# Hybrid RWKV-7 / GLA layer: the inverse of the 32x32 diagonal blocks moved from VectorE to GpSimd, with one packed transpose, and lower right-hand sides carried through a matmul by an identity

## Chip, cores and metric

One core of one Trainium2 chip. The metric is the device time of one execution of the whole program in microseconds, the median over several runs. What a run leaves beside the time is a profile of one execution.

## The reference

One decoder layer on 2048 tokens of width 1024: an RMS norm, one input projection of 3248 columns, two mixers side by side on its columns (RWKV-7 with 8 heads of 64, and gated linear attention with 4 heads), an output projection with residual, a second norm, a SwiGLU feed-forward network of width 2816 with residual, and a last norm. The change touches the RWKV-7 mixer, whose recurrence over the tokens is, for each head,

```python
def step(S, inp):
    r_t, w_t, k_t, v_t, a_t, b_t = inp
    sa = jnp.einsum('bhvk,bhk->bhv', S, a_t)
    S = (S * w_t[:, :, None, :] + sa[..., None] * b_t[:, :, None, :]
         + v_t[..., None] * k_t[:, :, None, :])
    y = jnp.einsum('bhvk,bhk->bhv', S, r_t)
    return S, y
```

with a decay `w`, `a = -kk` (the normed key) and `b = kk * iclr`. All of it is in fp32.

## The kernel before, in words

**Two phases.** Phase A (0 to about 1340 us) is the input projection and both mixers, in four blocks of 512 tokens. Phase B (`phase_b`) is the output projection and the feed-forward network; the change doesn't touch it.

**Phase A.** A block has 8 chunks of 64 tokens, and its 8 RWKV heads go in 4 head pairs, 128 channels to a pair: 16 pairs in the four blocks. Five streams of work exist: `z` (the projection: `weights` loads a 128-column tile of the weight and splits it, ScalarE writes the high part `w_hi` on L371 and GpSimd the low part `w_lo` on L372; `zmm` runs 24 matmuls into the PSUM tile `zd`, of which there are two; `shift` and `shifted` mix in the token before, with two small GpSimd copies on L390 and L393), `a` (`stage_a`: from r, k and v of a pair to the scores `e` and `ra`), `a2` (`stage_a2`, below), `b` (`stage_b`: the chain over a pair's 8 chunks, whose steps on VectorE are `uv` on L695 and two updates of the state `S` on L703) and `g` (the gated attention, `gmix`, with a copy of its state to `gss` on GpSimd, L822). Each stream is a generator that yields an estimated time after each piece of work; `run` merges the five by these times, and the framework's scheduler then settles the order of the instructions on each engine from the merged program. Within an engine the order is fixed when the program is built: an instruction that waits holds up all that stand behind it on that engine.

**Chunked form.** Within a chunk the recurrence is a triangular system: `I - E` with the 64x64 strictly triangular `E` of the scores has to be inverted and applied to the right-hand sides `R` (two halves: the scaled `a` and a product with `v`). For a pair there are 16 such matrices (8 chunks, 2 heads), in `e`. `stage_a2` treats each as 2x2 blocks of 32: it inverts the two diagonal blocks, and does a block substitution with matmuls.

**The inverse of the diagonal blocks (L597 to L626).** Four transposes on VectorE of 32x32 squares (L597, one for each group of 32 partitions) write `ln`; each reads the elements repeated four times, so that a lane has 1024 elements. Then `lm` is set to an identity by a GpSimd copy (L601), and 31 substitution steps follow, j from 31 down to 1. Each is two instructions on VectorE, `lt = lm[j] * ln` (L606) and `lm = lm + lt` (L608), on 128 lanes with j x (8 - j // 4) elements each; each needs the result of the one before it:

```python
for j in range(31, 0, -1):
    i0 = j // 4
    n = 8 - i0
```

After the step j = 8 the matmuls for the right-hand sides are issued (`atp`, L615, and `upp`, L622, whose results ScalarE copies into `R`). A VectorE transpose of `lm` then gives the inverses `ui` (L626).

**The block substitution.** X and R are the same tile. For the upper 32 rows of a chunk X = T R (matmuls `xu` on L640, ScalarE copies on L644). The upper rows, times the lower left block of `e` (matmuls `xy` on L648, contraction over 32 rows), are added to the lower rows of R by VectorE (L653). The lower rows are then multiplied by their own inverse (`xl` on L657, ScalarE copies on L661). At the end the part of X for `a` is transposed back (`wtp`) for `stage_b`.

Of the kernel before, what the change touches and what calls it, by code (L numbers as in the profile page):

```python
# [11 lines left out]
F32 = mybir.dt.float32  # L12
# [4 lines left out]
ALU = mybir.AluOpType  # L17
PSUM = bass.MemoryType.PSUM
DRAM = bass.MemoryType.DRAM

D = 1024
# [13 lines left out]
# column tiles of the input projection  # L35
ZR, ZK, ZV, ZL, ZG, ZQ, ZKG, ZVG, ZOG = 0, 4, 8, 12, 13, 14, 16, 18, 22

# columns of the per-channel vectors
# [3 lines left out]
# columns of the constant block  # L42
# [23 lines left out]
class K:  # L66
# [16 lines left out]
    def rsqrt(self, x, n, name):  # L83
        """1/sqrt(x) for a small [128, n] tile: integer first guess, three Newton steps."""
        nc = self.nc
        y = self.small.tile([128, n], F32, name=name + "_y")
        t = self.small.tile([128, n], F32, name=name + "_t")
        nc.vector.tensor_scalar(out=y.bitcast(I32), in0=x.bitcast(I32), scalar1=-0.5, scalar2=float(0x5F3759DF),
                                op0=ALU.mult, op1=ALU.add)
        for _ in range(3):  # L90
            nc.vector.tensor_tensor(out=t, in0=y, in1=y, op=ALU.mult)
            nc.vector.scalar_tensor_tensor(out=t, in0=t, scalar=-0.5, in1=x, op0=ALU.mult, op1=ALU.mult)
            nc.vector.scalar_tensor_tensor(out=y, in0=t, scalar=1.5, in1=y, op0=ALU.add, op1=ALU.mult)
        return y

    # A step y -> (x y y - 3 s s) y takes s / sqrt(x) to -2 s^3 / sqrt(x): the scales that end in 1.
# [4 lines left out]
    def row_rs(self, ss, keep=None):  # L101
        """1/rms of 128 rows from two partial sums of squares."""
        nc = self.nc
        x = self.small.tile([128, 1], F32, name="rn_x")
        nc.vector.tensor_tensor(out=x, in0=ss[:, 0:1], in1=ss[:, 1:2], op=ALU.add)
        nc.vector.tensor_scalar(out=x, in0=x, scalar1=1.0 / D, scalar2=RMS_EPS, op0=ALU.mult, op1=ALU.add)
        y = (keep or self.small).tile([128, 1], F32, name="rn_y", bufs=16 if keep else 2)
        t = self.small.tile([128, 1], F32, name="rn_t")
        nc.vector.tensor_scalar(out=y.bitcast(I32), in0=x.bitcast(I32), scalar1=-0.5, scalar2=-554047172.0,
                                op0=ALU.mult, op1=ALU.add)  # L110
        for sc in (self.S0, self.S1, self.S2):
            nc.vector.scalar_tensor_tensor(out=t, in0=x, scalar=y, in1=y, op0=ALU.mult, op1=ALU.mult)
            nc.vector.scalar_tensor_tensor(out=y, in0=t, scalar=-3.0 * sc * sc, in1=y, op0=ALU.add, op1=ALU.mult)
        return y

    def row_scale(self, x, junk, keep=None):
        """1/rms of the rows of a [128, D] tile."""
        nc = self.nc
        ss = self.small.tile([128, 2], F32, name="rn_ss")
        for i in range(2):  # L120
            nc.scalar.activation(out=junk, in_=x[:, i * 512:i * 512 + 512], func=AF.Square, accum_out=ss[:, i:i + 1])
        return self.row_rs(ss, keep)

# [1 line left out]
    def phase_a(self, ctx):  # L125
# [34 lines left out]
        # persistent state  # L160
# [21 lines left out]
    def stacks(self):  # L182
        nc = self.nc
        # up-projections: rows [hi; lo; hi] against data [hi; hi; lo] (and the like)
# [15 lines left out]
    def run(self):  # L200
        """Emits the blocks' work as streams that are merged by estimated time."""
# [27 lines left out]
    @staticmethod  # L229
    def some(gen, n):  # L230
        """The next n timed steps of a stream."""
        for r in gen:
            yield r
            n -= isinstance(r, float)
            if not n:
                return
# [37 lines left out]
    def xcols(self, b, kp):  # L274
        """256 columns of a block's rows."""
# [3 lines left out]
    def nstat0(self):  # L279
        """1/rms of the first block's rows, from the tiles that nprep goes on with."""  # L280
# [16 lines left out]
    def nstat(self, b):  # L297
        """1/rms of the block's rows."""
# [10 lines left out]
    def nprep(self, b):  # L309
        """the block's normed rows, channel-major, in hi and lo parts, 256 channels a tile."""  # L310
# [50 lines left out]
    def weights(self, ct):  # L361
        """128 columns of the input projection, in hi and lo parts."""
# [12 lines left out]
    def zmm(self, ct):  # L375
        """z^T of one 128-column tile of the input projection, [128, BLK] in PSUM."""
# [9 lines left out]
    def shift(self, ps, i, rows=128):  # L386
        """mu-weighted copy of z, one token late; the last column is kept for the next block."""
# [66 lines left out]
    def stage_a(self, b, hp):  # L454
        """From r, k, v of one head pair to everything that the chain over its chunks needs."""
# [12 lines left out]
        # decay  # L468
# [45 lines left out]
        # [b|k] (even chunk) and [k|b] (odd chunk), divided by the running decay  # L514
# [3 lines left out]
        # r and a of the two chunks, times the running decay; T a comes to the places before and after r  # L518
# [6 lines left out]
        # scores  # L525
# [18 lines left out]
        # token-major [b;k]  # L544
# [9 lines left out]
        # token-major centred v (chunks of a pair swapped)  # L554
# [13 lines left out]
        # bonus * v  # L568
# [17 lines left out]
    def stage_a2(self, b, hp):  # L586
        """Applies the inverse of I - E to the right-hand sides [a | A_ak v]."""
# [4 lines left out]
        # inverses of the 32x32 diagonal blocks of I - E, one per lane and four rows  # L592
        ln = s.tile([128, 32, 32], F32, name="ln", bufs=1)
        for q in range(4):
            par, t0 = q // 2, 32 * (q % 2)
            ev = e.rearrange("p h a x t -> p (h a) x t")[32 * q:32 * q + 32, :, par, t0:t0 + 32]
            nc.vector.transpose(out=ln[32 * q:32 * q + 32],  # L597
                                in_=ev.rearrange("p a t -> p t a").unsqueeze(2).to_broadcast([32, 32, 4, 8]))
# [4 lines left out]
        for j in range(31, 0, -1):  # L603
            i0 = j // 4
            n = 8 - i0
            nc.vector.tensor_tensor(out=lt[:, 0:j, i0:], in0=lm[:, j:j + 1, i0:].to_broadcast([128, j, n]),  # L606
                                    in1=ln[:, j, 0:j].unsqueeze(2).to_broadcast([128, j, n]), op=ALU.mult)
            nc.vector.tensor_tensor(out=lm[:, 0:j, i0:], in0=lm[:, 0:j, i0:], in1=lt[:, 0:j, i0:], op=ALU.add)  # L608
            yield 0.6
            if j == 8:  # L610
                # right-hand sides, token-major, pairs of chunks on the partitions
# [16 lines left out]
        # X = T R by blocks of 32  # L628
# [17 lines left out]
        for g in G2:  # L646
            ps = self.mb("xy", [128, 2, 2, 2, 64])
            each(ps, g, lambda ps, i, j, h, par: nc.tensor.matmul(  # L648
                out=ps[lw(par), i, :, h, :], lhsT=e[up(par), h, j, par, 32:64], rhs=X[up(par), j, :, h, :],
                start=True, stop=True))  # L650
            for par in range(2):
                Rg = R[lw(par), 2 * g:2 * g + 2]
                nc.vector.tensor_tensor(out=Rg, in0=ps[lw(par)], in1=Rg, op=ALU.add)  # L653
# [18 lines left out]
    def stage_b(self, b, hp):  # L672
        """The chain over the chunks of one head pair, group norm, bonus and gate."""
# [7 lines left out]
        for c in range(NCH):  # L681
# [10 lines left out]
            # T a S in the chunk's own rows, r S in the other rows  # L692
# [22 lines left out]
        # group norm (y is centred), gain, bonus, gate  # L715
# [84 lines left out]
    def gmix(self, b, jj):  # L800
# [4 lines left out]
        # token-major k  # L805
# [6 lines left out]
        # chunk states  # L812
# [18 lines left out]
        for h in range(2):  # L831
            hq = slice(64 * h, 64 * h + 64)
            # scores
# [41 lines left out]
    # tiles of phase B take the slots that phase A's tags leave  # L875
# [29 lines left out]
    def phase_b(self):  # L905
# [10 lines left out]
        def prep(half, nb, kps=range(KT // 2)):  # L916
            """normed rows of 512 tokens, channel-major, in hi and lo parts."""
# [25 lines left out]
        # output projection and residual  # L943
# [118 lines left out]
def layout(inp):  # L1062
    """Lays the inputs out for the kernel: tiles, padding and per-channel columns."""
# [60 lines left out]
```

## Time and profile before

| quantity | value |
|---|---|
| median of 3 runs | 3018.58 us (3017.28 to 3021.06) |
| span of the profiled execution | 3011.3 us |
| TensorE busy (matmuls) | 2871.0 us (95% of the span) |
| VectorE busy | 1732.7 us (58%) |
| ScalarE busy | 953.1 us (32%) |
| GpSimd busy | 344.2 us (11%) |
| DMA | 206.08 MB, 68 GB/s over the span |

The span is the time between the first and the last instruction in the profile of one execution; the times of the runs hold what lies around it as well. A share is an average over two phases that differ: of 40 slices of the span, the first 17 or 18 are phase A, with VectorE at six to eight tenths, and the rest phase B, with VectorE at three to five tenths and TensorE at nine or more. So a stage is to be read in its own stretch. PE is TensorE (PEld its loading of weights), DVE is VectorE, ACT ScalarE, POOL GpSimd, SP the engine that issues the DMAs. The clock is the granted share of TensorE's full clock.

### The profile page before, as it was taken

What the parts mean: (1) busy time and instruction counts of PE and PEld (TensorE: products, weight loads), DVE (VectorE), ACT (ScalarE), POOL (GpSimd) and SP (SyncE); (2) the same over time, 40 slices, a digit from 0 to 9 for tenths busy, and PEclk for the clock granted to TensorE, in tenths of its full rate; (3) what the DMA queues carried; (4) which work ended last, traced back from release to release, by engine and by line L of the source; (5) the groups of instructions that cost most, each with busy time, mean ns of one, the idle gap of its engine ahead of it and who ended that gap; (6) DMA issues with size and microseconds to landing.
All of it is one profiled execution on the core that took longest, in us unless ns stands there. A gap on an engine that the chain in (4) does not pass through costs nothing.

```text
span 3011.3 us, 38996 instructions
## 1 busy us (share of the span) xinstructions
PE 2871.0 (95%) x15112; PEld 2247.0 (75%) x15112; DVE 1732.7 (58%) x3990; ACT 953.1 (32%) x1718; POOL 344.2 (11%) x451
## 2 busy tenths in 40 slices
PE   7898999899898989899999999999999999999998
PEld 5676677666666767668878888888888888888886
DVE  6868797888888897874433333333355333333334
ACT  5444445444445445332321111111132111111112
POOL 4222232213322222200000000000000000000000
PEclk9999989989999999989999999999999999999999
DMA  3122111221122111135531111111134111111111
GB/s 108 48 71 78 50 53 47 78 67 56 53 67 81 53 53 50 57 114 175 180 119 45 54 42 42 50 55 50 42 126 138 52 42 42 51 54 50 42 42 57
DMA packets 99033, 206.08 MB, mean 68 GB/s; under 512 B 8608, under 2 KB 41600, under 8 KB 98848
## 3 DMA queue, kind: packets, MB, share of 16 engines
q1 hardware_dynamic: 98848, 203.59, 21.7%
q8 instruction: 119, 1.95, 0.3%
q14 instruction: 66, 0.54, 0.1%
HBM read 178.39 MB, written 25.17 MB: 68 GB/s over the span
## 4 chain that ended last, share of the span: by engine, by line
PE 76%; DVE 20%; issue 2%; ACT 1%; DMA 1%; POOL 0%; SPq 0%; DVEq 0%; ACTq 0%; POOLq 0%
PE ups L995 5%; PE ups L996 5%; PE gps L996 5%; PE gps L997 5%; PE gps L995 5%; PE ups L997 5%; PE dn L1018 5%; PE dn L1019 5%; PE dn L1017 5%; DVE ln L597 3%; PE zd L383 3%; DVE lm L608 3%; PE zd L381 3%; PE zd L382 3%; DVE lt L606 3%
## 5 line engine op out<-in xcount | busy, mean ns | idle before, releaser
L381 PE MATMUL zd<-nh,w_hi 128*128 128x512 f32 x832 | 353.9, 426 | 0.8 <-DVE gkk L777 0.6
L383 PE MATMUL zd<-nh,w_lo 128*128 128x512 f32 x832 | 349.2, 420 | 0.0
L1020 DVE TENSOR_TENSOR h<-dn,h 128x512 f32<-128x512 f32 x352 | 242.7, 690 | 180.6 <-PE dn L1019 180.5
L382 PE MATMUL zd<-nl,w_hi 128*128 128x512 f32 x832 | 345.6, 415 | 0.0
L372 POOL TENSOR_TENSOR w_lo<-w_raw,w_hi 128x512 fp32r<-128x512 f32 x208 | 273.8, 1322 | 614.5 <-ACT w_hi L371 571.8
L1000 DVE TENSOR_TENSOR sgu<-sgu,ups 128x512 f32<-128x512 f32 x88 | 60.2, 684 | 392.6 <-PE ups L997 390.4
L1018 PE MATMUL dn<-wdl,hh 128*128 128x512 f32 x704 | 278.4, 395 | 0.0
L996 PE MATMUL gps<-n2l,wgh 128*128 128x512 f32 x704 | 278.2, 395 | 0.0
L995 PE MATMUL gps<-n2h,wgh 128*128 128x512 f32 x704 | 277.6, 394 | 0.4 <-ACT wgh L901 0.4
L996 PE MATMUL ups<-n2l,wuh 128*128 128x512 f32 x704 | 278.0, 395 | 0.0
L995 PE MATMUL ups<-n2h,wuh 128*128 128x512 f32 x704 | 277.7, 394 | 0.2 <-ACT wuh L901 0.2
L1019 PE MATMUL dn<-wdh,hl 128*128 128x512 f32 x704 | 277.7, 395 | 0.0
L997 PE MATMUL gps<-n2h,wgl 128*128 128x512 f32 x704 | 277.4, 394 | 0.0
L997 PE MATMUL ups<-n2h,wul 128*128 128x512 f32 x704 | 277.4, 394 | 0.0
L1017 PE MATMUL dn<-wdh,hh 128*128 128x512 f32 x704 | 277.4, 394 | 0.0
L901 ACT CAST wdh<-raw 128x1024 fp32r<-128x1024 f32 x44 | 46.4, 1053 | 462.5 <-PE dn L1019 250.5
L383 PEld LDWEIGHTS zd<-nh,w_lo 128*128 128x128 f32 x832 | 161.6, 194 | 35.7 <-issue 7.5
L381 PEld LDWEIGHTS zd<-nh,w_hi 128*128 128x128 f32 x832 | 162.5, 195 | 33.2 <-issue 5.2
L382 PEld LDWEIGHTS zd<-nl,w_hi 128*128 128x128 f32 x832 | 161.9, 195 | 33.3 <-issue 7.9
L371 ACT CAST w_hi<-w_raw 128x512 fp32r<-128x512 f32 x208 | 126.3, 614 | 130.9 <-PE zd L382 83.7
L999 ACT ACTIVATE sgu<-gps 128x512 f32<-128x512 f32 x88 | 52.7, 599 | 339.4 <-PE gps L997 339.4
L995 PEld LDWEIGHTS gps<-n2h,wgh 128*128 128x128 f32 x704 | 132.1, 188 | 33.0 <-ACT wgh L901 0.9
(244 smaller groups left out, 5111.9 us busy)
## 6 DMA issues: line engine op xcount, KB each, us to landing
w_raw<-in_win SPq DMA_DIRECT2D x208, 256.0 KB, 2.7
raw<-in_wg SPq DMA_DIRECT2D x44, 512.0 KB, 4.2
raw<-in_wu SPq DMA_DIRECT2D x44, 512.0 KB, 3.6
raw<-in_wd SPq DMA_DIRECT2D x44, 512.0 KB, 3.6
xk<-in_x SPq DMA_DIRECT2D x16, 512.0 KB, 4.6
raw<-mix SPq DMA_DIRECT2D x16, 512.0 KB, 3.6
hx<-in_x SPq DMA_DIRECT2D x16, 512.0 KB, 3.6
hs<-hx SPq DMA_DIRECT2D x16, 512.0 KB, 2.9
```

What stands on the lines that cost most here:

```text
L371: nc.scalar.copy(out=whi[:, ks, :], in_=raw)
L372: nc.gpsimd.tensor_tensor(out=wlo[:, ks, :], in0=raw, in1=whi[:, ks, :].bitcast(F32), op=ALU.subtract)
L381: nc.tensor.matmul(out=ps, lhsT=whi[:, k, :], rhs=self.nh[k], start=(k == 0), stop=False)
L382: nc.tensor.matmul(out=ps, lhsT=whi[:, k, :], rhs=self.nl[k], start=False, stop=False)
L383: nc.tensor.matmul(out=ps, lhsT=wlo[:, k, :], rhs=self.nh[k], start=False, stop=(k == KT - 1))
L995: nc.tensor.matmul(out=ps, lhsT=w[0][:, ks], rhs=h, start=(k == 0), stop=False)
L996: nc.tensor.matmul(out=ps, lhsT=w[0][:, ks], rhs=l, start=False, stop=False)
L997: nc.tensor.matmul(out=ps, lhsT=w[1][:, ks], rhs=h, start=False, stop=(k == KT - 1))
L1017: nc.tensor.matmul(out=ps, lhsT=hh[:, ts], rhs=wd[f][0][:, ds], start=(f == 0), stop=False)
L1018: nc.tensor.matmul(out=ps, lhsT=hh[:, ts], rhs=wd[f][1][:, ds], start=False, stop=False)
L1019: nc.tensor.matmul(out=ps, lhsT=hl[:, ts], rhs=wd[f][0][:, ds], start=False, stop=(f == 1))
L1020: nc.vector.tensor_tensor(out=H[t][:, ds], in0=ps, in1=H[t][:, ds], op=ALU.add)
```

## The change

- The four transposes of a pair become one. ScalarE first copies the four diagonal squares into a packed tile `ed` (four copies of 32 partitions x 256 elements; `ed` takes the slot of `lt`), and one VectorE transpose on 128 lanes, which reads `ed` with the same fourfold repetition, writes `ln`.
- All 62 substitution instructions of a pair are issued on GpSimd; the operations, their operands and their order are the same.
- Two GpSimd copies for each pair write a 32x32 identity over the lower diagonal squares of `e`, once the squares are in `ed`. The matmul `xy` then contracts over all 64 rows of a chunk, the upper rows of X through the lower left block and the lower rows of R through the identity, so that its result is already the sum. ScalarE copies it into R, in place of VectorE's addition.

```diff
@@ -584,18 +584,24 @@
         yield (f"a1{b}.{hp}",)
     def stage_a2(self, b, hp):
         nc, s = self.nc, self.s
         yield f"a1{b}.{hp}"
         Pm, art, e, ra, bkt, uv, bv = self.ab.pop((b, hp))
         ars = art[:, 1:].rearrange("p (a x) t -> p a x t", x=4)
-        ln = s.tile([128, 32, 32], F32, name="ln", bufs=1)
+        ed = s.tile([128, 32, 8], F32, name="ed", tag="lt", bufs=1)
         for q in range(4):
             par, t0 = q // 2, 32 * (q % 2)
             ev = e.rearrange("p h a x t -> p (h a) x t")[32 * q:32 * q + 32, :, par, t0:t0 + 32]
-            nc.vector.transpose(out=ln[32 * q:32 * q + 32],
-                                in_=ev.rearrange("p a t -> p t a").unsqueeze(2).to_broadcast([32, 32, 4, 8]))
+            nc.scalar.copy(out=ed[32 * q:32 * q + 32], in_=ev.rearrange("p a t -> p t a"))
+        ln = s.tile([128, 32, 32], F32, name="ln", bufs=1)
+        nc.vector.transpose(out=ln, in_=ed.unsqueeze(2).to_broadcast([128, 32, 4, 8]))
+        for par in range(2):
+            q = slice(64 * par + 32, 64 * par + 64)
+            nc.gpsimd.tensor_copy(out=e.rearrange("p h a x t -> p (h a) x t")[q, :, par, 32:64],
+                                  in_=self.ident[q, q].unsqueeze(1).to_broadcast([32, 8, 32]))
         yield 4.0
         lm = s.tile([128, 32, 8], F32, name="lm", bufs=1)
         nc.gpsimd.tensor_copy(out=lm, in_=self.dlt.rearrange("p (k i) -> p k i", i=8))
@@ -603,12 +609,12 @@
         for j in range(31, 0, -1):
             i0 = j // 4
             n = 8 - i0
-            nc.vector.tensor_tensor(out=lt[:, 0:j, i0:], in0=lm[:, j:j + 1, i0:].to_broadcast([128, j, n]),
+            nc.gpsimd.tensor_tensor(out=lt[:, 0:j, i0:], in0=lm[:, j:j + 1, i0:].to_broadcast([128, j, n]),
                                     in1=ln[:, j, 0:j].unsqueeze(2).to_broadcast([128, j, n]), op=ALU.mult)
-            nc.vector.tensor_tensor(out=lm[:, 0:j, i0:], in0=lm[:, 0:j, i0:], in1=lt[:, 0:j, i0:], op=ALU.add)
+            nc.gpsimd.tensor_tensor(out=lm[:, 0:j, i0:], in0=lm[:, 0:j, i0:], in1=lt[:, 0:j, i0:], op=ALU.add)
             yield 0.6
             if j == 8:
                 R = s.tile([128, NPR, 2, 2, 64], F32, name="R", bufs=2)
                 atp = self.mb("atp", [128, NPR, 128])
                 for i in range(NPR):
@@ -625,7 +631,7 @@
         ui = s.tile([128, 8, 32], F32, name="ui", bufs=1)
         nc.vector.transpose(out=ui.rearrange("p a (i x) -> p i x a", x=4), in_=lm.rearrange("p k i -> p i k"))
         yield 0.5
         X = R
         up = lambda par: slice(64 * par, 64 * par + 32)
         lw = lambda par: slice(64 * par + 32, 64 * par + 64)
@@ -646,11 +652,10 @@
         for g in G2:
             ps = self.mb("xy", [128, 2, 2, 2, 64])
             each(ps, g, lambda ps, i, j, h, par: nc.tensor.matmul(
-                out=ps[lw(par), i, :, h, :], lhsT=e[up(par), h, j, par, 32:64], rhs=X[up(par), j, :, h, :],
-                start=True, stop=True))
+                out=ps[lw(par), i, :, h, :], lhsT=e[64 * par:64 * par + 64, h, j, par, 32:64],
+                rhs=X[64 * par:64 * par + 64, j, :, h, :], start=True, stop=True))
             for par in range(2):
-                Rg = R[lw(par), 2 * g:2 * g + 2]
-                nc.vector.tensor_tensor(out=Rg, in0=ps[lw(par)], in1=Rg, op=ALU.add)
+                nc.scalar.copy(out=R[lw(par), 2 * g:2 * g + 2], in_=ps[lw(par)])
             yield 1.5
         for g in G2:
             ps = self.mb("xl", [128, 2, 2, 2, 64])
```

Lines of the changed program have numbers that are 2 to 6 higher from `stage_a2` on (it also leaves out the comments): L599 is the packed transpose, L603 the identity copies, L612 and L614 the substitution, L632 the transpose to `ui`, L658 the copy that replaces the addition, L700 and L708 `stage_b`'s `uv` and `S`, L827 the copy of `gss`.

**How the order moves.** The first place is VectorE in the second block of tokens, second pair: behind the last score eviction of `stage_a` (`e`, `ra`). Before, this stretch has the end of the first pair's substitution with its `ui`, the four transposes of the second pair, and the beginning of the second pair's substitution:

```order
L606 TENSOR_TENSOR lt<-lm,ln 128x8
L608 TENSOR_TENSOR lm<-lm,lt 128x8
L597 STREAM_TRANSPOSE ln<-e 32x1024
L626 STREAM_TRANSPOSE ui<-lm 128x32x8
L597 STREAM_TRANSPOSE ln<-e 32x1024 x3
L606 TENSOR_TENSOR lt<-lm,ln 128x31
L608 TENSOR_TENSOR lm<-lm,lt 128x31
L653 TENSOR_TENSOR R<-xy,R 32x512 x4
L606 TENSOR_TENSOR lt<-lm,ln 128x30
L608 TENSOR_TENSOR lm<-lm,lt 128x30
L606 TENSOR_TENSOR lt<-lm,ln 128x29
```

In the changed program, from that eviction on, with the second pair's own `ui`:

```order
L539 TENSOR_TENSOR e<-scp,cst 128x4x64
L541 TENSOR_TENSOR ra<-scp,cst 128x256
L599 STREAM_TRANSPOSE ln<-ed 128x1024
L632 STREAM_TRANSPOSE ui<-lm 128x32x8
L700 TENSOR_TENSOR uv<-yp,R 64x128
L708 SCALAR_TENSOR_TENSOR S_1_101<-ch,Pm_120,st 64x64 x2
L700 TENSOR_TENSOR uv<-yp,R 64x128
L708 SCALAR_TENSOR_TENSOR S_0_100<-ch,Pm_120,st 64x64 x2
```

The packed transpose and the one of `ui` now stand directly behind one another, and the steps of `stage_b` (`uv`, `S`) come behind `ui`.

The second place is VectorE in the first pair of the same block, behind the score evictions. Before:

```order
L597 STREAM_TRANSPOSE ln<-e 32x1024 x2
L606 TENSOR_TENSOR lt<-lm,ln 128x31
L608 TENSOR_TENSOR lm<-lm,lt 128x31
L606 TENSOR_TENSOR lt<-lm,ln 128x30
L608 TENSOR_TENSOR lm<-lm,lt 128x30
L606 TENSOR_TENSOR lt<-lm,ln 128x29
L398 SCALAR_TENSOR_TENSOR r<-zd,om,sh 128x512
L580 TENSOR_TENSOR bv<-bp,v 128x4x64 x2
L695 TENSOR_TENSOR uv<-yp,R 64x128
L608 TENSOR_TENSOR lm<-lm,lt 128x29
L606 TENSOR_TENSOR lt<-lm,ln 128x28
L608 TENSOR_TENSOR lm<-lm,lt 128x28
```

In the changed program:

```order
L599 STREAM_TRANSPOSE ln<-ed 128x1024
L708 SCALAR_TENSOR_TENSOR S_1_113<-ch,Pm_122,st 64x64 x2
L398 SCALAR_TENSOR_TENSOR r<-zd,om,sh 128x512
L580 TENSOR_TENSOR bv<-bp,v 128x4x64 x2
L700 TENSOR_TENSOR uv<-yp,R 64x128
L708 SCALAR_TENSOR_TENSOR S_0_112<-ch,Pm_122,st 64x64 x2
L718 TENSOR_TENSOR y<-yp,y 64x256 x2
L724 TENSOR_REDUCE va<-ysq 128x8
L726 TENSOR_SCALAR va<-va 128x8
L88 TENSOR_SCALAR gn_y<-va 128x8
L632 STREAM_TRANSPOSE ui<-lm 128x32x8
L91 TENSOR_TENSOR gn_t<-gn_y 128x8
```

Here work of the projection (`r`), of `stage_a` (`bv`) and of `stage_b` stands between the packed transpose and `ui`.

The third place is GpSimd in the third pair of the same block. Before (memsets for `uv`, the low parts of weights, the state copy of the gated attention, and the carry of the token shift):

```order
L563 MEMSET uv 64x2x128
L372 TENSOR_TENSOR w_lo<-w_raw,w_hi 128x512
L822 COPY gss<-SG_118 128x128
L372 TENSOR_TENSOR w_lo<-w_raw,w_hi 128x512
L393 COPY cr<-sh 128x1
L372 TENSOR_TENSOR w_lo<-w_raw,w_hi 128x512
```

In the changed program:

```order
L603 COPY e<-ident 32x8x32
L562 MEMSET uv 64x2x128
L563 MEMSET uv 64x2x128
L372 TENSOR_TENSOR w_lo<-w_raw,w_hi 128x512
L603 COPY e<-ident 32x8x32
L827 COPY gss<-SG_118 128x128
L612 TENSOR_TENSOR lt<-lm,ln 128x31
L614 TENSOR_TENSOR lm<-lm,lt 128x31
L612 TENSOR_TENSOR lt<-lm,ln 128x30
L614 TENSOR_TENSOR lm<-lm,lt 128x30
```

The copy of `gss` stands ahead of the substitution, and weights' low parts stand around it.

## Rows read from the trace of the kernel before

**Rows 1.** The page, its first line
```profile
span 3011.3 us, 38996 instructions
```

**Rows 2.** Stretches: length, busy us (count) of PE, PEld, DVE, ACT, POOL, clock, DMA
```profile
60.00:1260.00 1200.00, 1097.76 (x7232) 823.12 (x7231) 983.82 (x2605) 552.43 (x1059) 318.55 (x397) 0.95 0.20 61
1260.00:1340.00 80.00, 71.61 (x465) 52.38 (x464) 60.79 (x184) 31.70 (x60) 0.61 (x2) 0.85 0.30 94
```

**Rows 3.** Busy time by stretches of 10 us, same columns
```profile
60.00:70.00 10.00, 8.23 (x59) 6.29 (x58) 9.96 (x17) 3.52 (x6) 5.41 (x5) 1.00 0.28 80
430.00:440.00 10.00, 6.14 (x40) 4.91 (x36) 9.86 (x22) 2.44 (x4) 3.60 (x3) 0.79 0.25 88
440.00:450.00 10.00, 10.00 (x41) 8.23 (x40) 8.32 (x20) 2.21 (x4) 1.96 (x3) 0.52 0.00 1
490.00:500.00 10.00, 10.00 (x87) 7.94 (x84) 4.88 (x16) 5.14 (x11) 3.23 (x6) 1.00 0.20 55
1240.00:1250.00 10.00, 9.78 (x86) 8.08 (x85) 9.16 (x19) 4.54 (x9) 3.19 (x3) 1.00 0.31 94
```

**Rows 4.** Waits, PE: us in total, times, longest us
```profile
PE ch L700 <- DVE uv L695: 32.4, 28, 2.7
PE scp L536 <- DVE lt L606: 10.2, 4, 3.9
```

**Rows 5.** VectorE groups: busy us, mean ns; by line: ns min/median/max, first, last
```profile
L606 DVE TENSOR_TENSOR lt<-lm,ln 128x60 f32<-128x60 f32 (+24 forms) x496 | 136.9, 276 | 10.8
L608 DVE TENSOR_TENSOR lm<-lm,lt 128x60 f32<-128x60 f32 (+24 forms) x496 | 136.3, 275 | 10.3
L608 DVE TENSOR_TENSOR lm<-lm,lt x496: 157/217/1346, 74.1 to 1318.2; 128x60 f32<-128x60 f32 x16, 128x28 f32<-128x28 f32 x12, 128x66 f32<-128x66 f32 x11, 128x48 f32<-128x48 f32 x10
L597 DVE STREAM_TRANSPOSE ln<-e x64: 1902/1977/2027, 64.5 to 1267.2; 32x1024 f32<-32x1024 f32 x64
L626 DVE STREAM_TRANSPOSE ui<-lm x16: 612/673/749, 113.1 to 1319.4; 128x256 f32<-128x256 f32 x16
L653 DVE TENSOR_TENSOR R<-xy,R x64: 683/691/699, 123.1 to 1331.8; 32x512 f32<-32x512 f32 x64
```

**Rows 6.** Timeline: start, length us
```profile
402.72 1.28 POOL L372 TENSOR_TENSOR w_lo<-w_raw,w_hi 128x512 fp32r<-128x512 f32 x1
402.75 1.33 DVE L608 TENSOR_TENSOR lm<-lm,lt 128x31 f32<-128x31 f32 x1
```

**Rows 7.** GpSimd, by line: ns min/median/max
```profile
L372 POOL TENSOR_TENSOR w_lo<-w_raw,w_hi x208: 1252/1282/2696, 13.8 to 1255.0; 128x512 fp32r<-128x512 f32 x104
L390 POOL COPY sh<-cr x56: 173/184/604, 2.8 to 1225.8; 128x1 f32<-128x1 f32 x52, 96x1 f32<-96x1 f32 x4
L601 POOL COPY lm<-cst x16: 398/400/481, 11.7 to 1244.4; 128x256 f32<-128x256 f32 x16
L822 POOL COPY gss<-SG x8: 288/293/293, 26.8 to 1205.3; 128x128 f32<-128x128 f32 x8
```

**Rows 8.** Timeline of GpSimd
```profile
2.89 0.30 POOL L562 MEMSET uv<- 64x256 f32 x1
3.23 0.31 POOL L563 MEMSET uv<- 64x256 f32 x1
```

**Rows 9.** ScalarE, by line: ns min/median/max
```profile
L322 ACT ACTIVATE xk<-xk,rn_y x28: 490/498/512, 14.0 to 979.2; 128x256 f32<-128x256 f32 x28
L644 ACT COPY R<-xu x64: 557/576/580, 115.5 to 1325.0; 32x512 f32<-32x512 f32 x64
L551 ACT COPY bkt<-bkp x32: 585/586/588, 67.9 to 1283.9; 128x512 f32<-128x512 f32 x32
```

**Rows 10.** Busy time of the tile zd alone: PE, PEld, DVE, ACT, clock, DMA
```profile
60.00:1260.00 1200.00, 665.85 (x2311) 419.84 (x2309) 60.58 (x96) 52.45 (x81) 0.95 0.20 61
```

**Rows 11.** VectorE groups: busy us, mean ns, idle
```profile
L539 DVE TENSOR_TENSOR e<-scp,cst 128x256 f32<-128x256 f32 x64 | 26.5, 414 | 8.8 <-PE scp L536 8.1
L695 DVE TENSOR_TENSOR uv<-yp,R 64x128 f32<-64x128 f32 x128 | 36.8, 288 | 37.7 <-PE yp L693 35.1
```

## The prediction

> **What bounds the kernel now.** The span is 3011.3 us [rows 1]; the three timed runs have a median of 3018.6, 7.3 more, which lies around the span. The busy time by stretches puts the change into the mixers' stretch: of its 1200 us TensorE is busy for 1097.8 and idle for 102.2, and over the 80 us of its tail for another 8.4 [rows 2]: 110.6 us are all that this change can give back in idle time. In stretches of 10 us one sees where they lie: where VectorE is busy for 9.9 of 10, TensorE falls to 6.1; where it is busy for 4.9, TensorE has its 10.0 [rows 3]. Of the 120 stretches between 60 and 1260 us, 54 have VectorE at 9.0 or more (the first and the last stand in rows 3); I added up TensorE's idle time in them: 70.2 of the 102.2 us, and 32.1 in the other 66. TensorE's waits name VectorE too, the second of the two shown the substitution itself [rows 4]. So VectorE is the near limit there, and the change takes work from it.
>
> **What it removes.** From VectorE: the transposes (64 x 1.977 = 126.5 us), both substitution lines (136.9 and 136.3) and the sums of the lower right-hand sides (64 x 0.691 = 44.2) [rows 5]: 443.9 of its 983.8 + 60.8 us there. It adds 16 packed transposes. A 32-lane one of the same width takes 1.98, and the 128-lane transpose of 256 elements 0.67, so 4 x 0.67 = 2.7 is the other bound [rows 5]; I take 1.98, the row of the same width, 32 us in all. Net, VectorE loses 412 us.
>
> **What it adds elsewhere.** ScalarE: 64 small copies at about 0.50 (a scaled copy of as many elements, SBUF to SBUF) and 64 copies of 32x512 at 0.576 [rows 9], 32 + 37 us on an engine busy for 552 of 1200 [rows 2]; only the last two small copies before a transpose lie on the path. TensorE: the matmuls that carry the identity have 64 rows for 32, in the same number; I cost that at nothing, since every matmul streams as many columns as before. GpSimd: 32 copies of 256 elements at 0.40 [rows 7], and the substitution.
>
> **The price of the substitution on GpSimd.** 62 instructions follow each other, each needing the one before, with j x (8 - j/4) elements each, 3120 in sum. No row shows a small two-input operation on GpSimd. The nearest: 1.252 for two inputs of 512 elements, 0.173 for a copy of 1, 0.398 for one of 256 [rows 7]; between two instructions that need each other 0.035 passes (2.89 + 0.305 to 3.23) [rows 7, 8]. Priced as copies: 62 x 0.208 + 3120 x 0.88 ns = 15.6 us. Priced with the copy's fixed part and the slope that leads to 1.252 (2.11 ns): 12.9 + 6.6 = 19.5 us. Priced as two copies each, which also meets 1.252 (2 x 0.624): 62 x 0.381 + 3120 x 1.76 ns = 29.1 us. I take 19.5: the row of the same operation, with the smallest addition; 15.6 and 29.1 are the ends.
> The Trainium skill (GPSIMD Engine Reference, Performance versus the Vector engine) gives 4497 ns for a two-input add of 2048 elements; with the 1252 of rows 7 that is 2.11 ns an element, the middle price and the middle sum, where the two-copy price would have 3950. No run here shows that size.
>
> **What stands around it.** On VectorE the 62 steps were spread between other work; in the new order VectorE has between the packed transpose and the one of ui, which waits for all 62, only 5.1 us of work in a block's first pair, none in the second, 7.9 and 5.8 in the third and fourth (durations of the rows of before). Then it stands, and all its work behind ui with it. Two w_lo steps (2.6 us) and up to 1.0 us of small fills stand inside the chain on GpSimd, so it lasts 23.1, 22.1, 22.4 and 22.1 us. Counted from the pair's last score matmul, it starts after the eviction of e (0.41), two copies (1.0), the transpose (1.98) and hand-overs of some 0.25 each: 4.4 us in the second pair [rows 5, 9, 11]. By the costs of a matmul of the next paragraph: in the first it starts at 5.4, since ScalarE has an eviction of 0.586 before its last copy, which waits for 2 projection matmuls and 14 other passes (1.8); in the fourth at 6.1, since VectorE has uv (0.29) before the transpose, behind 1 and 34 (3.3) [rows 9, 11]; in the third at 6.9, since GpSimd's copy of gss (0.29) stands ahead of the chain and waits for 2 and 66 (6.4), the last of them of the gated-attention stream [rows 7]. With ui (0.67 and a hand-over) the inverse is there at 29.3, 27.3, 30.1 and 29.0 us.
> How long can TensorE go on? In its queue stand, up to the first matmul that needs VectorE's work behind ui, 60, 56, 41 and 42 projection matmuls and 47, 130, 94 and 98 other passes (an fp32 matmul is two). A projection matmul costs 665.9 / 2311 = 0.288, another pass (1097.8 - 665.9) / 4921 = 0.088 [rows 2, 10]. That is 21.4, 27.6, 20.1 and 20.7 us, and VectorE needs 4.3, 0.3, 0.6 and 0.3 of it behind ui: ui is due at 17.1, 27.3, 19.5 and 20.4. **TensorE stands** 12.2, 0, 10.6 and 8.6 us, 31.4 a block, 126 over four blocks. The projection cannot fill this: it is in the count, and its two PSUM banks are drained by the engine that stands.
>
> **The sum.** Out go the 110.6 us of idle time; 32 stay, those of the stretches where VectorE was not full; 126 come: +47 us, 3058.7 for the span and, against the median, **3066 us**. The clock is 0.95 granted [rows 2]; a stretch with 3.9 us of idle time is followed by one at 0.52 [rows 3], and the new waits are fewer and longer than the old: I leave its loss as it is. Phase B has the same instructions. By the ends of the price, 15.6 brings 79 us of waits and 3019, 29.1 brings 279 and 3219.
>
> **Rivals.** (1) *Faster: the relief wins.* For it: 412 us less on VectorE, and the chain of some 22 us takes less than the interleaved one, which in the last pair ran from 1267 to 1319 us [rows 5]. If the chain is 15 us or less (copies' price), waits come to 79 or less; if the freed VectorE also leaves only 12 us of the old idle time, and a third of the clock's loss (5% of 1098 is 55) returns, that gives 3018.6 + 79 + 12 - 110.6 - 18 = 2981. It decides from a chain of about 15.6 us down. Against it: fixed part and gap alone are 12.9. (2) *Slower by far:* two-copy price, 3219. Against it: the plain slope meets the same row with less. (3) *The engines shut each other out.* A substitution step on VectorE took 1.33 beside a w_lo of GpSimd that began 0.03 earlier and ended 0.08 earlier, 0.157 at best [rows 5, 6]. If all of VectorE's work between transpose and ui holds the chain up, the chains are 5.1, 0, 7.9 and 5.8 longer, the waits 50 a block, 201 in all: 3141. Against it: VectorE stands for most of the chain, and work with an input in PSUM need not take part.
> The Trainium skill (SBUF — State Buffer, Who interferes with whom) says that a VectorE instruction with two SBUF inputs and a GpSimd one that reads SBUF exclude each other for whole instructions, whoever comes second waiting; by that rule 62 more such GpSimd instructions go into each pair, and rows 6 agree with it at 1.28 against 1.33. (4) *No change:* waits near 80 replace the old ones, 3015 to 3025: the low price with everything else as in the sum.
>
> **How the numbers follow.** The forecast, with prices from 17 to 24 us for the chain (3040 to 3115), has 0.45; rival 1 0.20; rival 2 0.15; rival 3 0.12; rival 4 0.08. Within 0.2%, 6 us, no measurement of this kernel tells it from no change. So faster 0.20, same 0.08, slower 0.72. The range goes from rival 1's value to short of rival 2's end: 2982 to 3200. The likeliest case's own range is 3040 to 3115.
>
> **What would show it.** Right: GpSimd's two-input steps at 0.2 to 0.35 us; VectorE idle for 15 to 22 us before ui, released by GpSimd; TensorE waiting 8 to 12 us, three times in a block, for VectorE work that stands behind ui; VectorE's busy time down by some 400 us. Wrong: no wait of TensorE above 4 us around ui, or steps of 0.15 us (then rival 1), steps of 0.45 (rival 2), or steps much longer than their minimum wherever VectorE works (rival 3).

## The result and the profile after

The changed kernel takes 3157.68 us, the median of 4 runs (3156.75 to 3158.49), beside 3017.93 for the kernel before on the same chip: a ratio of 1.047, with a 95% interval of 1.0453 to 1.0487. It is slower, by 140 us where 47 were forecast.

The first lines of the page of the changed kernel:

```profile
span 3156.5 us, 39043 instructions
PE 2881.6 (91%) x15112; PEld 2265.3 (72%) x15112; DVE 1377.7 (44%) x2886; ACT 1032.5 (33%) x1846; POOL 652.1 (21%) x1475
```

The span is 145.2 us longer than in [rows 1]. To see where, the same work has to be laid side by side: all of phase A up to the last transpose of X (`wtp`), whose end is at 1337.5 us before and at 1478.2 after. Busy time by stretches, with the columns of [rows 2], of the kernel before

```profile
0.00:1337.50 1337.50, 1209.02 (x7871) 907.35 (x7872) 1076.73 (x2844) 615.65 (x1182) 344.16 (x451) 0.94 0.22 65
```

and of the changed kernel

```profile
0.00:1478.20 1478.20, 1215.42 (x7855) 922.96 (x7856) 720.28 (x1740) 694.54 (x1309) 652.12 (x1475) 0.89 0.19 59
```

So 140.7 of the 145.2 us lie in phase A. TensorE is busy there for only 6.4 us more; its idle time goes from 128.5 to 262.8 us. VectorE's busy time falls by 356 us (by 406 if the lengths of its instructions are added up, which overlap a little at their ends), where 412 were counted. What has gone up is TensorE's waiting, while the engine that it waits for has less to do. The waits of TensorE and of VectorE in the changed kernel (us in total, times, longest):

```profile
PE ch L711 <- DVE S L708: 63.5, 14, 14.6
PE ytp L735 <- DVE y L730: 57.4, 8, 17.1
PE gsc L843 <- DVE gss L833: 42.7, 3, 14.4
PE ch L705 <- DVE uv L700: 41.2, 8, 13.7
DVE ui L632 <- POOL lm L614: 289.5, 16, 25.3
```

TensorE's four lines name four different pieces of VectorE's work, and none is the inverse: state steps, the norm of `stage_b`, the gated attention's state. The last line tells what they share: VectorE stands before `ui` in each of the 16 pairs, 18 us on average, for the last substitution step on GpSimd, and all these pieces stand behind `ui` in its queue. One such wait, in the first pair of the second block, in the timeline of the changed kernel (start, length; idle time before in brackets):

```profile
418.89 1.25 DVE L599 STREAM_TRANSPOSE ln<-ed 128x1024 f32<-128x1024 f32 x1 [1.52 <-ACT ed L597]
420.29 0.25 POOL L612 TENSOR_TENSOR lt<-lm,ln 128x31 f32<-128x31 f32 x1 [0.96 <-DVE ln L599]
430.78 0.17 DVE L88 TENSOR_SCALAR gn_y<-va 128x8 int32<-128x8 int32 x1
434.62 0.39 PE L382 MATMUL zd<-nl,w_hi 128*128 128x512 f32 x1
445.82 0.20 POOL L614 TENSOR_TENSOR lm<-lm,lt 128x8 f32<-128x8 f32 x1
446.06 0.67 DVE L632 STREAM_TRANSPOSE ui<-lm 128x256 f32<-128x256 f32 x1 [15.11 <-POOL lm L614]
447.19 1.26 POOL L372 TENSOR_TENSOR w_lo<-w_raw,w_hi 128x512 fp32r<-128x512 f32 x1
447.27 1.19 DVE L91 TENSOR_TENSOR gn_t<-gn_y 128x8 f32<-128x8 f32 x1
451.32 0.69 DVE L730 TENSOR_TENSOR y<-y,gn_y 128x512 f32<-128x512 f32 x1
452.06 1.12 PE L735 MATMUL ytp<-ident,y 128*128 128x128 f32 x4 [17.06 <-DVE y L730]
```

The scores end at 415.7. The chain runs on GpSimd from 420.3 to 446.0. VectorE has finished what was put ahead of `ui` at 430.95 and stands for 15.1 us. TensorE runs out of other work at 435.0; it needs `ytp`, which needs the norm (L88 to L730), whose second half is behind `ui`. It stands for 17.1 us.

The new instructions by line (ns min/median/max, first and last start):

```profile
L612 POOL TENSOR_TENSOR lt<-lm,ln x496: 204/278/318, 70.0 to 1420.0; 128x60 f32<-128x60 f32 x16, 128x28 f32<-128x28 f32 x12, 128x66 f32<-128x66 f32 x11, 128x48 f32<-128x48 f32 x10
L614 POOL TENSOR_TENSOR lm<-lm,lt x496: 204/321/376, 70.3 to 1420.3; 128x60 f32<-128x60 f32 x16, 128x28 f32<-128x28 f32 x12, 128x66 f32<-128x66 f32 x11, 128x48 f32<-128x48 f32 x10
L599 DVE STREAM_TRANSPOSE ln<-ed x16: 1234/1246/1247, 68.6 to 1396.3; 128x1024 f32<-128x1024 f32 x16
```

The packed transpose takes 1.25 us, less than the 32-lane one of the same width in [rows 5] (1.98).

### The profile page after: what moved, and what is told of

The parts are those of the page before. It is cut to its first block, busy times and chain, and to the rows that moved or that the text cites. A ratio compares the mean times of both kernels' runs of the same rounds, so it can differ in the third digit from the quotient of the medians.

```text
span 3156.5 us, 39043 instructions
## 1 busy us (share of the span) xinstructions
PE 2881.6 (91%) x15112; PEld 2265.3 (72%) x15112; DVE 1377.7 (44%) x2886; ACT 1032.5 (33%) x1846; POOL 652.1 (21%) x1475
## 4 chain that ended last, share of the span: by engine, by line
PE 75%; POOL 11%; DVE 7%; issue 4%; ACT 3%; DMA 1%; POOLq 0%; SPq 0%; DVEq 0%; ACTq 0%
PE ups L1000 5%; PE ups L1001 5%; PE gps L1001 5%; PE gps L1002 5%; PE gps L1000 5%; PE ups L1002 5%; PE dn L1023 5%; PE dn L1024 5%; PE dn L1022 5%; POOL lm L614 5%; POOL lt L612 4%; PE zd L383 3%; PE zd L381 3%; PE zd L382 3%; PE op L969 2%
## 5 line engine op out<-in xcount | busy, mean ns | idle before, releaser
L614 POOL TENSOR_TENSOR lm<-lm,lt 128x60 f32<-128x60 f32 (+24 forms) x496 | 153.4, 309 | 36.9
```

Of the source, the lines that this page charges most:

```text
L614: nc.gpsimd.tensor_tensor(out=lm[:, 0:j, i0:], in0=lm[:, 0:j, i0:], in1=lt[:, 0:j, i0:], op=ALU.add)
```

## The experiments

Each ran beside the kernel before; the ratio is to that kernel's runs, with its 95% interval. Diffs are cut to the edit.

**1. The parts, one at a time.** First the changed kernel without its GpSimd part:

```diff
-            nc.gpsimd.tensor_tensor(out=lt[:, 0:j, i0:], ...
-            nc.gpsimd.tensor_tensor(out=lm[:, 0:j, i0:], ...
+            nc.vector.tensor_tensor(out=lt[:, 0:j, i0:], ...
+            nc.vector.tensor_tensor(out=lm[:, 0:j, i0:], ...
```

> The changed kernel with the 62 substitution steps of each pair back on VectorE; packed transpose, ScalarE copies and identity stay. Theory A (VectorE stands at the transpose to ui for the chain on GpSimd, 15 to 25 us in each of 16 pairs, and TensorE behind it for 207 us in all): the waits go, VectorE keeps the 150 us that the other two parts take from it, so faster than before, 2960 to 3000 us. Rival B (the identity part, its 64-row matmuls and its copies on ScalarE, is what costs): stays above 3060. Rival C (GpSimd and VectorE shut each other out on memory): as A, and it does not tell the two apart by its time; VectorE's steps that meet w_lo would still take 1.3 us.

Measured: 3013.67 us, ratio 0.9999 (0.9984 to 1.0015). The waits at `ui` for the chain are gone, so the loss sits in the GpSimd part; but the gain that theory A expected of the rest did not come.

The reverse, the kernel before with only these two lines turned to `nc.gpsimd`:

> The kernel before with nothing but the 62 substitution steps of each pair moved to GpSimd; four 32-lane transposes and the additions on VectorE stay. Theory A: the waits for the chain are there as in the changed kernel, and each pair's inverse starts later by the longer transposes (4 x 1.98 for 1.25 us, some 3 to 6 us net), so 3150 to 3230 us. Rival B (identity part): near 3018, at most 3060.

Measured: 3154.41 us, ratio 1.0465 (1.0439 to 1.049), the whole loss by itself. Its trace also has steps that meet a VectorE instruction. In its timeline:

```profile
82.75 1.23 DVE L488 TENSOR_TENSOR_SCAN cum<-scn,cum 128x512 f32<-128x512 bf16 x1
82.96 1.16 POOL L608 TENSOR_TENSOR lm<-lm,lt 128x66 f32<-128x66 f32 x1
```

The 66-element step, 0.34 us elsewhere, lasts until VectorE's scan is over (84.12 and 83.98 us). Six of the 992 steps are longer than 0.4 us here, five of them 0.61 to 1.23, and none in the changed kernel.

The identity part alone, on the kernel before:

```diff
+        for par in range(2):
+            q = slice(64 * par + 32, 64 * par + 64)
+            nc.gpsimd.tensor_copy(out=e...[q, :, par, 32:64], in_=self.ident[q, q]...)
-                lhsT=e[up(par), h, j, par, 32:64], rhs=X[up(par), j, :, h, :]
+                lhsT=e[64 * par:64 * par + 64, h, j, par, 32:64], rhs=X[64 * par:64 * par + 64, j, :, h, :]
-                nc.vector.tensor_tensor(out=Rg, in0=ps[lw(par)], in1=Rg, op=ALU.add)
+                nc.scalar.copy(out=R[lw(par), 2 * g:2 * g + 2], in_=ps[lw(par)])
```

> The kernel before with nothing but the identity in e, the matmul xy over 64 rows and ScalarE's copies for VectorE's 64 additions of 0.691 us. Theory A: VectorE loses 44 us where it is the near limit; 2995 to 3020 us. Rival B: 3060 or more.

Measured: 3047.47 us, ratio 1.0107 (1.0077 to 1.0137). A miss for theory A: 33 us slower, with 44 us of additions taken off VectorE. And the packed transpose alone:

```diff
+        ed = s.tile([128, 32, 8], F32, name="ed", tag="lt", bufs=1)
-            nc.vector.transpose(out=ln[32 * q:32 * q + 32], in_=ev...)
+            nc.scalar.copy(out=ed[32 * q:32 * q + 32], in_=ev.rearrange("p a t -> p t a"))
+        nc.vector.transpose(out=ln, in_=ed.unsqueeze(2).to_broadcast([128, 32, 4, 8]))
```

> The kernel before with nothing but the packed tile (four ScalarE copies of 0.64 us a pair) and the one transpose of 1.25 us on 128 lanes for the four of 1.98. Theory A: VectorE loses 126 - 20 = 106 us where it is the near limit; TensorE has 132 us of idle time in phase A, part of which returns: 2960 to 3010 us. Rival B says nothing of it; if ScalarE's copies come late and hold the transpose up, 3010 to 3030.

Measured: 2988.35 us, ratio 0.9912 (0.9881 to 0.9942), as theory A had it. The four runs add up within 8 us: the packed transpose gives 26 us, the identity part takes 33, and the two together (the first run) take 1 us off; GpSimd's part costs 140 by itself and some 142 on top of the others.

**2. Where in the identity part.** Two runs on the kernel before. One has the 64-row matmul, with zeros in place of the identity, and VectorE's additions (the fill is `nc.gpsimd.memset(e...[q, :, par, 32:64], 0.0)`):

> The kernel before with xy over 64 rows, where the lower diagonal squares of e hold zeros, written by two GpSimd fills a pair; VectorE's additions stay. Tells what of the identity part's 33 us is the matmul's. Theory G (the 64 rows, or the wait for what is written into e, cost TensorE's time or clock): 3030 to 3050 us. Rival H (the cost is in ScalarE's copies, or in the order that comes out of them): 3010 to 3025.

The other has the 32-row matmul and ScalarE's copies, and leaves the sum of the lower right-hand sides out:

```diff
-                nc.vector.tensor_tensor(out=Rg, in0=ps[lw(par)], in1=Rg, op=ALU.add)
+                nc.scalar.copy(out=R[lw(par), 2 * g:2 * g + 2], in_=ps[lw(par)])
```

> The kernel before with xy over 32 rows, and ScalarE's copy of the product into R in place of VectorE's addition: the addition of the lower right-hand sides is left out. VectorE loses 44 us, ScalarE gains 37. Theory G: 2990 to 3015 us, the gain that the identity part was to bring. Rival H: 3030 to 3050.

Measured: 3016.21 us, ratio 1.0021 (1.0007 to 1.0036) with the zero rows, and 3031.35, ratio 1.0068 (1.0052 to 1.0084) with the copies. So most of it comes with the copies, as rival H had it, and some 6 us with the rows or the fills. A run of 16 `xy` passes (8 matmuls of the program) takes 1.06 us with 32 rows and with 64. TensorE's waits for the score evictions are longer with the identity part,

```profile
PE scp L536 <- DVE ra L541: 19.6, 12, 4.5
```

and with the copies alone,

```profile
PE scp L536 <- DVE ra L541: 21.0, 11, 4.5
```

where the kernel before has

```profile
PE scp L536 <- DVE ra L541: 6.4, 6, 3.5
```

In all, though, TensorE's idle time is only 6 us longer than before (134.5 and 128.5): most of the 33 us is busy time. Up to the last `wtp` TensorE is busy for 1237.72 us with the identity part (same columns as above), against 1209.02, at a granted clock of 0.92 for 0.94:

```profile
0.00:1372.20 1372.20, 1237.72 (x7866) 934.66 (x7867) 1041.86 (x2785) 656.29 (x1247) 361.23 (x483) 0.92 0.21 63
```

By the clock's records in the trace, 212 us of that busy time were run at the lower of the two granted levels (0.50, 1.2 GHz), against 142 in the kernel before: at half speed the 70 us more are worth 35 us, as much as the whole part costs. Taking the additions off VectorE changes the order that the scheduler builds on every engine; the zero rows leave VectorE's and ScalarE's order as it was. Whether the copies or that order cost the time was not separated, nor why the clock was lower for longer.

**3. The place of `ui`, or the length of the chain?** In the changed kernel, `ui` is queued behind all VectorE work that the merged program has ahead of it:

```diff
+        yield 0.1
+        last = next(i for i in reversed(nc.cur_bb.bb.instructions) if i.engine == mybir.EngineType.DVE)
+        with self.tc.issue_after(last):
             nc.vector.transpose(out=ui..., in_=lm...)
```

> The changed kernel with one difference: the transpose to ui is issued on VectorE behind all the VectorE work of the other streams that comes ahead of it in the merged program, so that 20 to 70 instructions stand between the packed transpose and ui where the changed kernel has 0 to 30. Theory A (the cost is the place of ui: VectorE stands and holds the state steps and the norm behind it): VectorE's wait at ui falls from 289 us to under 60, TensorE's waits above 4 us from 218 us to under 60, time 2990 to 3050 us. Rival D (the cost is the length of the chain: the inverse comes too late for its own matmuls, wherever ui stands): TensorE then waits at xu and what follows, time stays above 3120. Rival C (port exclusion): with VectorE at work beside the chain GpSimd's steps grow from 0.30 us to 0.6 and more, and the time stays above 3100.

Measured: 3055.47 us, ratio 1.0142 (1.0123 to 1.0161): about 100 us of the loss are gone, and VectorE never waits for the chain at `ui`. The inverse comes later still, 47 to 63 us behind the scores where the changed kernel has 29 to 39, and no `xu` matmul is among TensorE's larger waits: rival D falls. So does rival C: with VectorE at work beside the chain the median step takes 0.295 us, for 0.294 in the changed kernel, though 23 of the 992 now take over 0.4 us, up to 1.33. The time is 5 us above the range, for the largest wait of TensorE is now another one:

```profile
PE zd L383 <- POOL w_lo L372: 59.4, 15, 8.7
```

The projection's low weights stand behind the chain in GpSimd's queue. The next run shortens the chain, in the changed kernel, by leaving steps out:

```diff
         for j in range(31, 0, -1):
+            if 8 < j < 24:
+                yield 0.6
+                continue
```

> The changed kernel without the substitution steps j = 9 to 23: 30 of a pair's 62 instructions on GpSimd are left out, so that the inverse is incomplete. By their rows these take some 30 x (0.31 + 0.08) = 11.5 us a pair. Theory A (each us of the chain is a us in which TensorE stands, once its cover is used up): 15 to 17 us waits of TensorE fall to 4 to 6, the 7 us waits to 0; 207 us of waits fall to some 55 and the time to 2995 to 3025 us. Rival D predicts the same here. A theory in which the chain's length does not set the time would leave it above 3100.

Measured: 3029.41 us, ratio 1.0062 (1.0042 to 1.0083). Some 125 us less, for 30 instructions fewer in a pair; VectorE's waits at `ui` are 154 us for 289:

```profile
DVE ui L635 <- POOL lm L617: 88.1, 12, 9.2
DVE ui L635 <- PE xl L665: 66.0, 4, 19.1
```

Only the 88 us are for the chain now. In the second pair of each block `ui`, a tile with one buffer, waits for the `xl` matmuls of the pair before, which still read it; there the chain has ended 1.9 to 6.9 us earlier. So with `ui` where the changed kernel has it, the length of the chain does set the time, as theory A had it, until this other wait takes over; the time is 4 us above its range.

**4. Taking the next victim away too.** The late `ui` without the identity part (diffs as above):

> As the run with the late ui, and without the identity part (additions back on VectorE, xy over 32 rows, no GpSimd copies into e). By the first runs the identity part alone costs 33 us and, on top of the packed transpose, 25: with theory A 20 to 40 us less than the run with the late ui, 2960 to 3020.

Measured: 3029.28 us, ratio 1.0054 (1.0037 to 1.0071), 26 us less, as expected, though 9 us above the end of the range. TensorE's wait for `w_lo` is the largest here as well, 61.9 us. So the low weights go to VectorE, which has room now:

```diff
-            nc.gpsimd.tensor_tensor(out=wlo[:, ks, :], in0=raw, ...
+            nc.vector.tensor_tensor(out=wlo[:, ks, :], in0=raw, ...
```

> The kernel with packed transpose, GpSimd substitution, late ui and VectorE additions, with the low parts of the weights (208 of 128x512) moved from GpSimd to VectorE, at about 0.69 us each by VectorE's row of the same shape, 143 us. Theory E (with ui late, the chain's next victim is the w_lo that stands behind it on GpSimd: 62 us of TensorE's waits): these waits go, VectorE rises to some 930 us of 1300, below the 1067 of the kernel with the packed transpose alone: 2955 to 2990 us. Rival F (VectorE is near its limit again): w_lo waits behind VectorE's work and the time stays at 3010 to 3040.

Measured: **2925.34 us**, ratio 0.9716 (0.9701 to 0.973), 86 us faster than the kernel before, and better than theory E's range. The stretch up to the last `wtp` (columns as above) of the run before this one, with `w_lo` on GpSimd, and of this one, and the largest wait of TensorE in this one:

```profile
0.00:1354.00 1354.00, 1203.86 (x7876) 907.08 (x7877) 744.20 (x1814) 659.11 (x1248) 638.81 (x1443) 0.93 0.21 65
0.00:1254.30 1254.30, 1176.98 (x7876) 896.02 (x7877) 845.21 (x2022) 658.53 (x1248) 426.88 (x1235) 0.96 0.23 70
```

```profile
PE ytp L735 <- DVE y L730: 24.1, 7, 6.6
```

TensorE's idle time is 77.3 us, against 128.5 before and 262.8 in the changed kernel; its busy time is 32 us less than before, at a clock of 0.96 for 0.94. Against the run with `w_lo` on GpSimd its idle time falls by 73 us, 62 of them the wait that theory E named, and its busy time by 27, which the theory did not count: 88 us of it are run at a granted clock of 0.50, for 140 there. With every second half tile of `w_lo` still on GpSimd (`(nc.gpsimd if i else nc.vector).tensor_tensor(out=wlo...)`):

> As the run with the low parts on VectorE, but only the first half of each weight tile there (104 of 208, 72 us), the second half on GpSimd. Theory E: half of the w_lo still stands behind the chain, since a tile needs both halves: 2990 to 3025 us. Rival F: better than with all of them on VectorE.

Measured: 2994.62 us, ratio 0.994 (0.9924 to 0.9957); TensorE waits 48.6 us for the half on GpSimd. Last, `w_lo` on VectorE in the changed kernel, with nothing else:

> The changed kernel with one difference: the low parts of the weights (208 of 128x512) are made on VectorE in place of GpSimd; ui stays where the order of the changed kernel has it. Theory A (VectorE stands at ui, and the chain's length prices each wait): the chains lose the w_lo that stand inside them, 2.5 to 5 us a pair, VectorE gets some work that may stand ahead of ui, and the rest of the waits, 10 to 13 us, stays: 3050 to 3120 us, far above the 2925 of the run that has the late ui as well. If w_lo alone was the trouble (Theory E alone), the time falls to 2950 to 2990, 25 to 40 above that run for the identity part.

Measured: 3094.35 us, ratio 1.0267 (1.0243 to 1.0291). The waits of TensorE and VectorE:

```profile
PE ch L711 <- DVE S L708: 113.1, 19, 14.4
DVE ui L632 <- POOL lm L614: 190.3, 16, 14.6
```

The wait at `ui` falls by 99 us, and the rest stays. Only 15 of the 99 come with shorter chains: these lose the two `w_lo` inside them, but 54 of the 992 steps now take over 0.4 us, up to 0.88. VectorE has 42 us more of work between the packed transpose and `ui`. Both corrections are needed: alone, they leave the kernel slower than before (1.0142, or 1.0054 without the identity part, and 1.0267 with it), together, without the identity part, they make it faster. Of the 2.8% the packed transpose gives 0.9 by itself.

## Why the prediction was right and wrong

**Right: direction and mechanism.** VectorE was forecast to stand before `ui` for the chain, with TensorE behind it for work that has nothing to do with the inverse. Experiment 3 shows it by moving `ui` alone. The forecast's bound for steps (0.2 to 0.35 us) holds but for the longest: they take 0.204 to 0.376. VectorE's waits before `ui` are 14.5 to 25.3 us, where 15 to 22 were forecast. The old idle time is gone as counted: beside the 207 us below and 17.7 in the first 60 us, 38 of the 262.8 us remain, where 32 were to stay.

**The step that failed: "TensorE stands 12.2, 0, 10.6 and 8.6 us, 31.4 a block, 126 over four blocks".** Added up in the timelines from the end of each pair's scores to 6 us behind `ui`, TensorE stands for 207 us, 81 more than the 126. With 6 us more of other idle time and 6 us of busy time they are the difference between the 47 forecast and the 140 measured. In the second block TensorE's longest waits are 17.1, 6.9, 14.6 and 14.3. Three terms under it were off:

- *The chain.* It was priced at 19.5 us alone. The last pair's, which has nothing else in it, takes 22.9 (from 1397.6 to 1420.5). Its steps take 18.1 us where the price had 17.3. Its hand-overs take 0.08 each where 0.035 was read off two fills: these write different rows of `uv`, so they don't need each other, though the prediction said they did. With `w_lo` and small copies or fills inside, the other chains take 25.0 to 25.8 us instead of 22.1 to 23.1.
- *Its start in the third pair.* The chain was to start 6.9 us behind the scores, after GpSimd's copy of `gss`. It began 13.0 us behind them (9.3 to 13.0 over the four blocks). The packed transpose itself stood behind a state step and `bv` in VectorE's queue and ended 10.7 us behind the scores; the copy, which waited for the last `gop` matmuls as foreseen, took 2.3 us more, and in the first block it came behind the chain's start. Part of the delay goes with TensorE's granted clock, 0.50 (1.2 GHz) from 580.6 to 594.3, after TensorE had stood for 2.8 of the 6.6 us before; in the third block it was 1.00, and the chain began at 9.3. In the second pair, with nothing ahead, it began 3.6 to 4.7 us behind the scores, where 4.4 was forecast: the packed transpose took 1.25 us for 1.98, each of ScalarE's small copies 0.64 for 0.50.
- *How long TensorE goes on.* It was to need VectorE's held work after 21.4, 27.6, 20.1 and 20.7 us. The timelines have 19.3, 22.7, 24.9 and 18.4. The projection matmuls in the way are as many as counted (60, 56, 41 and 42), at 0.26 to 0.28 us for 0.288; of other passes the trace has 39, 110, 82 and 82 for 47, 130, 94 and 98. So in three pairs the cover ran out 2 to 5 us sooner. In the third it lasted longer by the lower clock, as the chain began later: the wait is 14.6 us there, and the same in the third block, where the cover was 21.2. Behind `ui`, the norm took 5.3 us for 4.3, since its small steps met `w_lo`, as the 1.19 us of L91 above.

These errors are small against the 25 us of a chain. But TensorE's wait is what is left of the chain after the cover, so 2 to 5 us on both sides make 22 us more on the 31.4 of a block (17.1, 6.9, 14.6 and 14.3 are 52.9).

**The rivals.** Rival 3 gave 3141 us, nearest to the result, but by luck: it had VectorE's work hold the chain up, and no step of the changed kernel took more than 0.376 us. VectorE stood for most of the chain, which is what the prediction held against it. The mechanism itself is there, as the scan of 1.23 us beside the step of 1.16 shows, and it grows as VectorE works beside the chain: in the fastest run (2925.34 us) 141 of the 992 steps take over 0.4 us, up to 1.40. The Trainium skill (SBUF — State Buffer, Who interferes with whom) has a VectorE instruction with two SBUF inputs and a GpSimd one that reads SBUF exclude each other for whole instructions; by the scan's rows, with both inputs in SBUF, the trace agrees. Rival 2's price of two copies is refuted by the steps' times. From 8 to 76 elements they rise from 0.20 to 0.31 and 0.35 us, so by 1.6 ns an element for L612 and 2.1 for L614, against the 2.11 taken. The Trainium skill (GPSIMD Engine Reference, Performance versus the Vector engine) has the 4497 ns from which the prediction estimated the same 2.11; the trace agrees with it for L614, and L612 is below. Rival 1 needed a chain of 15 us, and the shortest took 22.9.

**The identity part was costed at nothing on TensorE, and its 44 us on VectorE as a gain.** The matmul's price held (1.06 us for 16 passes either way). But the part by itself costs 33 us, which no step of the sum allowed for. In the changed kernel it does not show in the time, since beside the packed transpose, which gives 26 us, the two come to 1 us (the first run).

## What to carry to other kernels

A chain of dependent steps on an idle engine is not free if an in-order engine has to take up its result: look at what stands behind the instruction that waits, there, and behind the chain on its own engine. Move both out of the way (the consumer late, the other work off the chain's engine) before judging the offload: here the move by itself cost 4.7%; with both, and with the packed transpose, which alone gives 0.9%, the kernel is 2.8% faster than before. A wait is the remainder of two long times, so price both by rows of their own kind, hand-overs included, and expect the remainder to be off by more than either.

## What was not expected of the hardware

A hand-over from one GpSimd step to the next that needs its result takes 0.08 to 0.09 us, twice that from one queued fill to another [rows 8]. One 128-lane transpose of 1024 elements a lane takes 1.25 us, less than one on 32 lanes that reads the strided scores (1.98); whether the lanes or the strides make the difference was not separated. The kernel before and the one with the identity part have as many TensorE passes (15112) and idle times in phase A that are 6 us apart, yet differ by 33 us: TensorE's busy time at a granted clock of 0.50 is 142 us in the one and 212 in the other.
